# The modulation's side products in a two-branch mixer kernel: two channel tiles at every second large product instead of one at every product

## The chip, the cores and the metric

The kernel runs on one core of a Trainium2 chip. The metric is device microseconds (us) of one execution from launch to end. The kernel before has been timed three times: median 3220.7 us, 3216.38 to 3223.29 us.

A core has five engines with an instruction stream each: TensorE (PE in the profile, with its weight loads as PEld), VectorE (DVE), ScalarE (ACT), GpSimd (POOL) and SyncE (SP, which here issues nearly all DMAs). They wait for each other through semaphores. TensorE writes its results to PSUM, from where DVE and ACT fetch them.

## The reference, cut to what matters

Two layers over 384 tokens (128 of a prompt, 256 of a sample) with 2048 channels. In each layer the conditioning vectors give shift, scale and gate of the layer ("the modulation"), the normalised input goes through one large input projection, two branches mix the tokens, and a merged output projection ends the layer:

```python
mod_ctx = (jax.nn.silu(c_ctx) @ w_mod[l] + b_mod[l])[None]
mod_lat = jax.nn.silu(c) @ w_mod[l] + b_mod[l]
shift, scale, gate = jnp.split(mod, 3, axis=-1)
h = rms_norm(x, lp['g_pre']) * (1 + scale[:, None]) + shift[:, None]
(r, k, v, z_a, wlo_f, wlo_b, alo_f, alo_b, q_b, k_b, v_b, z_b, beta_in, alpha_in,
 gate_a_in, gate_b_in) = split_in_proj(h @ lp['w_in'])
# branch A: RWKV-7, 16 heads of 64, both directions     branch B: gated DeltaNet, 8 heads of 128
merged = sigmoid(gate_a_in) * branch_a + sigmoid(gate_b_in) * branch_b
out = merged @ lp['w_o']
x = x + gate[:, None] * rms_norm(out, lp['g_post'])
```

What the change concerns is `silu(c) @ w_mod[l]`: a product of two vectors (prompt and sample) with a matrix of 2048 x 6144 per layer.

## The kernel before

Large products take float32 operands as two float16 parts and multiply in three passes. A slab of 128 output channels of a weight matrix (1 MB, tile `st`) is loaded by SP, split into two `w` tiles by ACT and DVE (L228 to L230), and multiplied as 16 contraction tiles by 3 passes, 48 matmuls into a PSUM tile `jps`. `dense` (L446) goes through such tasks one after the other, always with the next slab loaded and split ahead, and calls `side_step(steps)` when a task's products have been issued.

The modulation is the side work that `side_step` (L349) takes up. `mod_third` (L277) is a generator for a third of it (shift, scale or gate of one layer). Each of its first 32 steps takes a `wm` tile (512 KB, two buffers, L347), issues its load (L285), and multiplies the 128 channels in it with the two conditioning vectors: four matmuls, each with a stationary `cpad` of 32 columns and 256 float32 columns streaming, into four 32-row groups of the PSUM tile `acc`. After the 32 steps ACT copies `acc` to a `wm` tile (L292); for thirds 0 and 1 four transposes follow, for third 2 the gate's rows go through DVE (L301, L302) to DRAM. 128 such steps are taken beside the large products: third 2 of layer 0, thirds 1 and 0 of layer 1 during layer 0, and third 2 of layer 1 during layer 1. In layer 0 61 tasks of branch A and 38 of branch B carry a step. `side_step(1000)` at the end of branch B takes whatever is left.

Branch A works through eight pairs of heads (0 to 7 below). Each has many short dependent products, written as generators too (`rwkv_front`, `rwkv_corner`, `rwkv_back`, `rwkv_out`); branch B has the same form with one head at a time. TensorE's order is made by `weave` (L91) as the program is written. It keeps a clock `now`, which every emitted matmul moves on by a planned cost (`mm`, columns / 2.4 ns, four times as much for float32, so 427 ns for a matmul of the side work). A generator yields how long its results need (HOP 1100, EVAC 2000, 3 * HOP and so on) or an event's name, and is taken up again when `now` is past that; in between come products of the `dense` tasks, which look up every second contraction tile. So side work on TensorE moves the generators' places. The orders of ACT, DVE, POOL and SP follow from a scheduler that works from priorities and dependencies, and which PSUM buffer a tile gets is settled there too; `tps`, the tile of most short products, has two.

Names in the rows: `k`, `r`, `v` are a pair's projections. `bones,sq` sums k's squares per head, `rs` is the inverse root of it (DVE L172, then POOL L173), `ident,rs` spreads it over the channels, `kk` (DVE L639) is k normalised, `lo,wup` are low-rank decays, `u` their evacuation on ACT (L651). `ivw`, `ivt` are the inversion of 32 x 32 blocks on DVE (L542 to L554), 60 short operations and two transposes to `nA` and `iva`. `nA,xc`, `iva,GA` and `v,revh` are products with the inverses and with v. In branch B `S,KQ`, `rt,Uf`, `vh,ktok`, `vn,QK` are the steps of the scan.

Of the kernel before, what the change touches and what calls it, by code (L numbers as in the profile page):

```python
# [24 lines left out]
# Large products: float32 operands are split exactly into float16 high and low parts after a power-of-two scaling;  # L25
# three passes (high high, high low, low high) carry float32's accuracy. Powers for weights, layer input, branches, merged.
SW, SX, SY, SM = 14, 6, 4, 4
# What TensorE's threads allow for, in ns: one answer of another engine (and a slower one, in those), a slab's way out of
# PSUM, convolution, decays, the first decays of branch B, inversions.
HOP, HOP_V, EVAC, CONV, DECAY, FIRST_B, INVERT_A, INVERT_B = 1100, 1.2, 2000, 8000, 7000, 3000, 37000, 48000  # L30
# Threads' ranks for the other engines; contraction tiles between two looks for a thread that can go on.
RANKS, STEP = (2000, 1000, 0, 0, 0, 0), 2
# By layer. Merge gates' channel tiles by pair of heads (and after the last) in branch A, by pair in branch B; branch A's
# projection by pair; the first heads of branch B that the last tiles of it take along; whole tiles left for the end.
# [5 lines left out]
# the order of the last outputs (block, slab), the residual's steps and those of the next input, by block  # L40
LAST = ("o00 o01 r0 r0 r0 o10 r0 o11 r1 r0 r1 o20 n0 r1 o21 r1 r2 n0 r2 n0 r2 r1 n0 r2 w0 w1 n1 n1 r2 w0 n2 n2 n2 "
        "n0 n0 n1 n1 n2 p0 n2 n2 w0 n0 n0 n0 n1 n1 n2 p0 n2 n2 w1 n0 n0 n0 n1 n1 n2 p0 p1 n2 n2 w1 p0 p1 p1 p1")
# channel tiles of the first modulation's pieces; the columns of the slabs that are multiplied piece by piece
# [7 lines left out]
def backbone(ctx: ExitStack, tc: tile.TileContext, i, o):  # L51
# [20 lines left out]
    # Work with many short dependent products is emitted by threads (generators). What a thread yields is the time, by the  # L72
    # cost of the products emitted meanwhile, that its results need before its next products, or the name of an event.
# [17 lines left out]
    def weave(threads, last):  # L91
        """Emits the threads' work; of those that can go on, the first does."""
# [33 lines left out]
    # each half reversed  # L126
# [5 lines left out]
    # sums the four groups of 32 rows  # L132
# [71 lines left out]
    def flag():  # L204
        """The column that takes a low part's sum: neither infinite (overflow) nor tiny everywhere (underflow)."""
        n = n_flag[0]
        n_flag[0] += 1
        return flags[:, n:n + 1]

    def run(fast):  # L210
# [21 lines left out]
        def weights(*srcs):  # L232
            """srcs [k 128, n] in DRAM -> their parts [128, all k, n] on chip"""
            return finish(weights_in_steps(*srcs))
# [22 lines left out]
        def product(ps, lhs, rhs, nk, ks=None):  # L257
            """ps += sum over k (of ks among nk) of lhs(part, k)^T rhs(part, k), in passes"""
            for kt in ks or range(nk):
                for n, (a, b) in enumerate(passes):  # L260
                    mm(ps, lhs(a, b, kt), rhs(a, b, kt), start=(kt == 0 and n == 0), stop=(kt == nk - 1 and n == len(passes) - 1))
                if kt % STEP == STEP - 1:
                    yield 0

        def finish(g):
            """runs a thread alone; its result"""
            try:
                while True:
                    next(g)
            except StopIteration as e:  # L270
                return e.value

# [4 lines left out]
        def mod_third(l, st, third, take):  # L277
            """One third of the modulation, half by half of its columns; take() gives the tile that they are loaded to."""
# [14 lines left out]
            if third == 2:  # L293
                # the gate's row, with the post-norm's weights, by streams
# [24 lines left out]
        def mod_piece(l, st, k0, k1, take):  # L319
            """Some channel tiles of shift and scale."""  # L320
# [27 lines left out]

        def side_step(n=1):  # L349
            while n and side:  # L350
# [7 lines left out]
        mods, pars = [], []  # L358

        def params(l):  # L360
# [25 lines left out]
            # halves; the rows of the output gates take the scale of their inputs as well  # L386
# [5 lines left out]
            # shift, scale by [channel, third, tile, stream]  # L392
# [4 lines left out]
        def norm_scale(ss):  # L397
            """ss[:, 0] = the norm's scale from two halves' sums of squares"""
# [6 lines left out]
        def scales(par, mod, ks):  # L405
            """the modulation's scales with the pre-norm's weights, in place"""
            V.scalar_tensor_tensor(out=mod[:, 1, ks], in0=mod[:, 1, ks], scalar=1.0, in1=bc(par[:, R_GPRE:R_GPRE + KT][:, ks], 2), op0=ADD, op1=MULT)

        def first_input(xT, par, mod, xs, kt):
            """layer 0: modulated channel tile, all tokens"""  # L410
# [5 lines left out]
        def layer(l, par, cw, hpar, omka, xs, ready, next_start, after):  # L416
# [5 lines left out]
            def by_channel(ws, n=128):  # L422
                """[channel, token] of a slab"""
# [6 lines left out]
            def by_token(ws):  # L430
                """[token in block, (block, channel)] of a slab"""
# [7 lines left out]
            def dense(tasks):  # L439
                """tasks: (slab, work with its parts); the next slab is loaded and split ahead"""  # L440
# [7 lines left out]
            def gate_tile(n):  # L448
                """tanh of half a channel tile of the merge gates, kept in DRAM"""
# [17 lines left out]
            # [token in block, (dir, head), block]  # L467
            beta, g, neg, vhs, al, ab = (lay.tile([128, 16, 3], F32, tag=t, name=t) for t in ("beta", "g", "neg", "vhs", "al", "ab"))
            # e^{cumulated g}; the same with the two chunks of a block swapped; e^{g left to the chunk's end}; e^{sum} of each chunk
# [18 lines left out]
            def decays():  # L488
# [34 lines left out]
                # neg: -e^g (forward), -beta e^g (backward); vhs: beta ekd (forward), ekd (backward)  # L523
# [7 lines left out]
            def silu2(ps, bufs=2):  # L531
                """2 silu(x) / cx from x / cx in PSUM"""
# [5 lines left out]
            def invert(pool, n_t):  # L538
                """n_t [128 = 4 quadrants of 32 rows, 32 blocks, 32]: minus a strictly upper N (row, column).
                Returns (a1, a2): a1[row, block, column] = (I + N)^-1, in n_t's place, and a2 its transpose, block by block."""  # L540
# [16 lines left out]
            # ================= branch A: RWKV-7, two heads per channel tile =================  # L557
# [4 lines left out]
            def lora(n):  # L562
                """a slab of the four low-rank inputs, each 96 channels"""
# [34 lines left out]
            def rwkv_tasks(hp):  # L598
                """the pair's projections; what a thread may still read is not overwritten before"""
# [19 lines left out]
            def rwkv_front(hp):  # L619
# [25 lines left out]
                # Z by chunk: rows of the solution (until then the k part of its right-hand side) and of the values  # L645
                kds, dirs, Zs = [], [], []
                for d in range(2):
# [28 lines left out]
                    # [channel, block, slot, 64]; slots of the even chunk then of the odd one:  # L676
                    # AR: r alpha | alpha r, BK: k b | b k; the backward direction has alpha, b and k reversed in time
# [27 lines left out]
                    # masked scores [row slot s, head, parity, block, t]: GA for alpha's columns, GR for r's  # L705
# [37 lines left out]
                # inverses: 32-blocks (the corner of each 64-block follows)  # L743
                a1, a2 = invert(P, nA)
                event(("inverse", l, hp), INVERT_A)
                # bonus: sum over the head's channels of r k r_k, both directions
# [12 lines left out]
            def rwkv_corner(hp):  # L759
# [3 lines left out]
                # the inverses of the 64-blocks, negated  # L763
# [22 lines left out]
            def rwkv_back(hp):  # L786
# [6 lines left out]
                # chunk by chunk; y takes the place of a chunk's alpha and r  # L793
# [78 lines left out]
                # bonus, group norm over the head, gate  # L872
# [665 lines left out]
```

## Time and profile before

| | |
|---|---|
| median of three runs | 3220.7 us (3216.38 to 3223.29) |
| the profiled execution, first to last instruction | 3223.1 us; it lists no time around this span |
| mean granted clock of TensorE | 0.969 |
| PE busy | 3009.9 us, 93% |
| DVE, ACT, POOL busy | 2325.1 (72%), 1461.4 (45%), 136.2 us (4%) |
| DMA | 457.89 MB, 142 GB/s in the mean |

The busy times are those of each engine alone, and overlap. TensorE is busy nearly always, so the span is TensorE's own work plus the short times in which it waits. Branch A of layer 0 lies at about 137 to 930 us, its branch B at 930 to 1470, branch A of layer 1 at 1690 to 2490 (with side work to 2096).

### The profile page before, as it was taken

The numbers are of one execution on the slowest core, as the hardware profiler recorded it, in microseconds if no ns is written. First come the engines' busy times: TensorE is split into PE (matmuls) and PEld (weight loads), VectorE is DVE, ScalarE is ACT, GpSimd is POOL, SyncE is SP. The second block draws the span as 40 slices with busy tenths as digits, with TensorE's granted clock in tenths as the row PEclk, the third lists the DMA queues.
The fourth block names the chain that finished last, engine by engine and source line by source line (L and its number), as shares of the span: only waits on it lengthen the run. The fifth ranks groups of instructions, "written<-read, shape, count | busy, mean of one in ns | idle before, by whom it ended". The sixth has DMA issues, their size and how long they took to land. (4 is left out here: it accounts for less than half of the span.)

```text
span 3223.1 us, 70249 instructions
## 1 busy us (share of the span) xinstructions
PE 3009.9 (93%) x28531; PEld 1990.2 (62%) x28531; DVE 2325.1 (72%) x6012; ACT 1461.4 (45%) x3144; POOL 136.2 (4%) x198
## 2 busy tenths in 40 slices
PE   6899999999999999997979999999999999999798
PEld 2466666666665555554976666666666655565388
DVE  3268888888867876765354788887887778887544
ACT  3344444444444555443355444444443446564332
POOL 1000000000000000000000000000000000000000
PEclk8999999999999999998989999999999999999899
DMA  9854444444465335467455545433334442335555
GB/s 342 263 147 132 125 126 133 140 131 139 135 173 159 108 113 159 139 185 201 126 158 156 141 132 149 114 99 91 98 106 123 118 127 71 106 89 167 152 150 160
DMA packets 659018, 457.89 MB, mean 142 GB/s; under 512 B 28858, under 2 KB 627708, under 8 KB 657148
## 3 DMA queue, kind: packets, MB, share of 16 engines
q1 hardware_dynamic: 658684, 453.30, 48.8%
q8 instruction: 227, 3.72, 0.5%
q14 instruction: 107, 0.88, 0.1%
HBM read 421.74 MB, written 31.49 MB: 141 GB/s over the span
## 5 line engine op out<-in xcount | busy, mean ns | idle before, releaser
L78 PE MATMUL jps<-x,w 128*128 128x384 f16 x8640 | 1534.3, 329 | 14.3 <-ACT x L228 7.9
L78 PEld LDWEIGHTS <-w 128*128 128x128 f16 (+1 forms) x10368 | 974.8, 99 | 735.0 <-issue 119.6
L230 DVE SCALAR_TENSOR_TENSOR w<-st,w 128x1024 f16<-128x1024 f32 (+3 forms) x574 | 643.9, 1128 | 239.5 <-ACT w L228 236.5
L228 ACT ACTIVATE w<-st 128x1024 f16<-128x1024 f32 (+3 forms) x574 | 556.3, 978 | 529.4 <-PE jps L78 333.6
L78 PE MATMUL cps<-w,mg 128*128 128x128 f16 x4608 | 265.0, 221 | 11.0 <-ACT mg L228 4.7
L78 PEld LDWEIGHTS <-mg 128*128 128x128 f16 x4608 | 263.6, 99 | 12.7 <-ACT mg L228 5.2
L549 DVE TENSOR_TENSOR ivw<-ivw,ivt 128x30 f32<-128x30 f32 (+4 forms) x720 | 237.6, 330 | 16.4
L547 DVE TENSOR_TENSOR ivt<-ivw 128x30 f32<-128x30 f32 (+4 forms) x720 | 236.8, 329 | 15.7
L78 PE MATMUL jps<-yb,w 128*128 128x384 f16 x744 | 138.9, 337 | 23.1 <-ACT w L228 11.9
L78 PE MATMUL jps<-ya,w 128*128 128x384 f16 x768 | 141.5, 333 | 4.3 <-ACT Uf L1291 1.8
L78 PE MATMUL acc<-wm,cpad 128*32 128x256 f32 (+1 forms) x1664 | 125.6, 384 | 16.0 <-DMA wm<-in_w_mod 15.9
L78 PEld LDWEIGHTS <-x 128*128 128x128 f16 x2304 | 131.3, 98 | 12.7 <-issue 10.0
L78 PE MATMUL jps<-w,x 128*128 128x128 f16 x2304 | 137.1, 220 | 0.0
L867 ACT COPY AR<-cps 64x128 f32<-64x128 f32 x192 | 49.9, 260 | 168.1 <-PE cps L78 163.5
L78 PE MATMUL tps<-AR,BK 64*128 64x128 f32 x768 | 119.0, 288 | 1.3 <-DVE GR L717 1.1
L1340 ACT ACTIVATE os<-cps,gx 64x128 f32<-64x128 f32 x160 | 57.9, 362 | 135.3 <-DVE rt L1338 132.9
L78 PEld LDWEIGHTS tps<-AR,BK 64*128 64x128 f32 x768 | 94.8, 187 | 20.0 <-issue 9.5
L840 DVE COPY Z<-cps 64x128 f32<-64x128 f32 x192 | 55.3, 288 | 60.6 <-PE cps L78 56.8
L730 ACT ACTIVATE nA<-GA 32x192 f32<-32x192 f32 x128 | 46.1, 360 | 108.0 <-DVE GA L715 106.7
L857 DVE SCALAR_TENSOR_TENSOR sring<-cps,pl,sp 64x64 f32<-64x64 f32 x256 | 72.4, 283 | 19.7 <-PE cps L78 15.4
L78 PEld LDWEIGHTS acc<-wm,cpad 128*32 128x32 f32 x1664 | 36.2, 110 | 71.2 <-issue 42.3
L1375 DVE SCALAR_TENSOR_TENSOR S<-S,gx,cps 128x128 f32<-128x128 f32 x128 | 39.1, 343 | 55.7 <-PE cps L78 55.3
(354 smaller groups left out, 3598.8 us busy)
## 6 DMA issues: line engine op xcount, KB each, us to landing
st<-in_w_in SPq DMA_DIRECT2D x194, 1024.0 KB
wm<-in_w_mod SPq DMA_DIRECT2D x176, 512.0 KB
st<-in_w_o SPq DMA_DIRECT2D x32, 1024.0 KB
st<-in_w_pa SPq DMA_DIRECT2D x32, 512.0 KB
gates<-gt SPq DMA_DIRECT2D x64, 192.0 KB
ms<-gates SPq DMA_DIRECT2D x64, 192.0 KB
st<-in_w_pb SPq DMA_DIRECT2D x36, 256.0 KB
wm<-in_w_mod SPq DMA_DIRECT2D x32, 256.0 KB
```

Of the source, the lines that this page charges most:

```text
L78: PE.matmul(out, lhsT=lhsT, rhs=rhs, start=start, stop=stop, **kw)
L228: S.activation(out=dst[0], in_=src, func=AF.Copy, scale=scale)
L230: V.scalar_tensor_tensor(out=dst[1], in0=src, scalar=scale, in1=dst[0], op0=MULT, op1=SUB, accum_out=flag())
L547: V.tensor_tensor(out=tv, in0=W[:, j + 1:32, j:j + 1].to_broadcast([128, n, j]), in1=W[:, j:j + 1, 0:j].to_broadcast([128, n, j]), op=MULT)
L549: V.tensor_tensor(out=W[:, j + 1:32, 0:j], in0=W[:, j + 1:32, 0:j], in1=tv, op=ADD)
L730: S.mul(nA[rq, 6 * d:6 * d + 6, :].rearrange("p (h b) t -> p h b t", h=2), GA[rq, :, p, :, 32 * q:32 * q + 32], -1.0)
L840: V.tensor_copy(dirs[d][4][ar, b, p, :], pb[ar, 0:128])
L857: V.scalar_tensor_tensor(out=sn[hs, hs], in0=pb[hs, o0:o0 + 64], scalar=plc[hs], in1=sp[hs, hs], op0=MULT, op1=ADD)
L867: S.copy(AR[rr, b, 2 * p:2 * p + 2, :].rearrange("p a b -> p (a b)"), pas[d][rr, 0:128])
L1340: S.activation(out=os_[d][R_, b, :], in_=pas[d][R_, 0:128], func=AF.Copy, scale=egs[R_, x, b:b + 1])
L1375: V.scalar_tensor_tensor(out=new[d], in0=cur[d], scalar=glast[:, p, x, b:b + 1], in1=pas[d][:, 128:256], op0=MULT, op1=ADD)
```

## The change

`side_step` now counts the steps that it is asked for in `owed`, returns while fewer than two are owed, and else takes all of them at once. Nothing else in the program differs (comments and docstrings are gone too, and lines behind the change are numbered higher by 7).

```diff
+        owed = [0]
+
         def side_step(n=1):
+
+            owed[0] += n
+            if owed[0] < 2:
+                return
+            n, owed[0] = owed[0], 0
             while n and side:
                 try:
                     next(side[0])
                     n -= 1
                 except StopIteration:
                     side.pop(0)
```

The same 512 matmuls of the side work stand in TensorE's order (before: 128 groups of four; now: 62 groups of eight and four of four). A pair of heads has seven tasks with a step, so from one pair to the next the groups fall behind other tasks.

The first place is TensorE in pair 3 of layer 0, from the sum of k's squares to the low-rank decays. Before:

```order
L78 MATMUL tps<-bones,sq 128x2 x3
L78 LDWEIGHTS w_4429
L78 MATMUL jps<-x_198,w_4429 128x384
...
L78 MATMUL tps<-ident,rs 64x128 x6
...
L78 MATMUL acc<-wm,cpad 32x256 x4
L78 LDWEIGHTS x_198
L78 MATMUL jps<-w_4494,x_198 128x128
...
L78 MATMUL tps<-lo,wup 128x384 x2
```

And now:

```order
L78 MATMUL tps<-bones,sq 128x2 x3
L78 LDWEIGHTS w_4429
L78 MATMUL jps<-x_198,w_4429 128x384
...
L78 MATMUL acc<-wm,cpad 32x256 x8
L78 MATMUL tps<-ident,rs 64x128 x6
L78 MATMUL tps<-lo,wup 128x384 x2
L78 LDWEIGHTS x_198
L78 MATMUL jps<-w_4488,x_198 128x128
```

Before, 24 large matmuls stand between `bones,sq` and `ident,rs`, then six, the side step and six more ahead of `lo,wup`. Now 18 large matmuls and two side steps stand ahead of `ident,rs`, and `lo,wup` follows it at once. Pairs 1, 5 and 7 read like 3; in pairs 2, 4 and 6 the side steps stand elsewhere, and 12 large matmuls and 42 more lie between `ident,rs` and `lo,wup`.

The second place is DVE at the same time, around `kk`. Before:

```order
L547 TENSOR_TENSOR ivt<-ivw 128x58
L639 SCALAR_TENSOR_TENSOR kk<-k,par,tps 128x384
L549 TENSOR_TENSOR ivw<-ivw,ivt 128x2x29
L547 TENSOR_TENSOR ivt<-ivw 128x30
L549 TENSOR_TENSOR ivw<-ivw,ivt 128x30
L553 STREAM_TRANSPOSE nA<-ivw 128x32x32
L554 STREAM_TRANSPOSE iva_4350<-ivw 128x32x32
L766 TENSOR_SCALAR Uf<-nA,m_122 128x12x32 x2
L230 SCALAR_TENSOR_TENSOR w_4578,flags<-st,w_4577 128x1024 x2
L659 SCALAR_TENSOR_TENSOR c_4599<-reset,u 128x384
```

And now:

```order
L554 TENSOR_TENSOR ivt<-ivw 128x58
L556 TENSOR_TENSOR ivw<-ivw,ivt 128x2x29
L554 TENSOR_TENSOR ivt<-ivw 128x30
L556 TENSOR_TENSOR ivw<-ivw,ivt 128x30
L560 STREAM_TRANSPOSE nA<-ivw 128x32x32
L561 STREAM_TRANSPOSE iva_4344<-ivw 128x32x32
L773 TENSOR_SCALAR Uf<-nA,m_122 128x12x32 x2
L230 SCALAR_TENSOR_TENSOR w_4569,flags<-st,w_4568 128x1024 x2
L646 SCALAR_TENSOR_TENSOR kk<-k,par,tps 128x384
L666 SCALAR_TENSOR_TENSOR c_4592<-reset,u 128x384
```

`kk`, which frees a `tps` buffer, has moved behind the end of the inversion, two transposes, two `Uf` and two splits of weights. It is so in pairs 1 and 3 of both layers.

The third place is TensorE at the end of layer 0's branch B. Before:

```order
L78 MATMUL cps<-S,KQ 128x128 x2
L78 MATMUL cps<-rt,Uf 64x128 x2
L78 MATMUL cps<-vn,QK 64x128 x2
L85 MATMUL tps<-swp,os 128x128 x3
L85 MATMUL tps<-ident,wm 128x128 x4
L78 LDWEIGHTS w_16662
L78 MATMUL jps<-yb_11081,w_16662 128x384
```

And now:

```order
L78 MATMUL cps<-S,KQ 128x128 x2
L78 MATMUL cps<-rt,Uf 64x128 x2
L78 MATMUL cps<-vn,QK 64x128 x2
L85 MATMUL tps<-swp,os 128x128 x3
L78 MATMUL acc<-wm,cpad 32x256 x4
L85 MATMUL tps<-ident,wm 128x128 x4
L78 LDWEIGHTS w_16634
L78 MATMUL jps<-yb_11093,w_16634 128x384
```

Layer 0 asks for 99 single steps, an odd number, so the last step of layer 1's third 0 is taken by `side_step(1000)`, and the transposes of this third stand right behind it.

## Rows read from the trace of the kernel before

**Rows 1.** The page: busy time, share of the span and instructions of each engine.
```profile
PE 3009.9 (93%) x28531; PEld 1990.2 (62%) x28531; DVE 2325.1 (72%) x6012; ACT 1461.4 (45%) x3144; POOL 136.2 (4%) x198
```

**Rows 2.** Windows by stage; columns are span, busy time per engine, PEclk, DMA share, GB/s.
```profile
137.00:930.00 793.00, 769.09 (x7484) 503.64 (x7485) 639.81 (x1640) 351.24 (x677) 38.75 (x39) 0.99 0.49 140
930.00:1470.00 540.00, 513.11 (x3958) 305.90 (x3956) 398.96 (x1055) 275.77 (x664) 22.30 (x22) 0.97 0.49 142
1690.00:2096.00 406.00, 394.57 (x3817) 260.52 (x3815) 310.18 (x775) 183.85 (x344) 18.09 (x30) 1.00 0.49 138
```

**Rows 3.** Tile `acc` on PE from 137 us: releaser, us of waiting, times.
```profile
  DMA wm<-in_w_mod: 2.2, 1
```

**Rows 4.** Timeline of PE: start, duration, instructions, [idle before, releaser].
```profile
400.30 7.97 PE L78 MATMUL jps<-x,w 128*128 128x384 f16 x48
408.20 0.64 PE L78 MATMUL acc<-wm,cpad 128*32 128x256 f32 x8
408.77 3.10 PE L78 MATMUL jps<-x,w 128*128 128x384 f16 x18
411.71 0.73 PE L78 MATMUL tps<-bones,sq 128*128 128x2 f32 x6
```

**Rows 5.** Timeline of PE early in layer 0: six side steps in a row.
```profile
87.51 2.80 PE L78 MATMUL acc<-wm,cpad 128*32 128x256 f32 x48
```

**Rows 6.** Waits of PE, 137 to 930 us: total us, times, longest.
```profile
PE tps L78 <- POOL rs L173: 6.7, 6, 1.3
PE tps L78 <- ACT v L609: 5.8, 7, 1.8
PE tps L78 <- ACT xc L775: 5.1, 12, 1.1
PE tps L78 <- DVE kk L639: 2.2, 6, 0.4
```

**Rows 7.** Timeline of PE in pair 3 of layer 0.
```profile
417.47 0.87 PE L78 MATMUL tps<-ident,rs 128*64 128x128 f32 x12 [1.11 <-POOL rs L173]
...
421.50 0.91 PE L78 MATMUL tps<-lo,wup 96*128 96x384 f32 x2 [0.36 <-DVE kk L639]
```

**Rows 8.** Timeline of DVE, the same stretch.
```profile
420.83 0.61 DVE L639 SCALAR_TENSOR_TENSOR kk<-k,par,tps 128x384 f32<-128x384 f32 x1
...
428.74 1.00 DVE L659 TENSOR_TENSOR_SCAN c<-reset,u 128x384 f32<-128x384 f32 x1
```

**Rows 9.** Timeline of ACT, the same stretch.
```profile
421.58 0.57 ACT L651 ACTIVATE u<-tps,hpar 128x384 f32<-128x384 f32 x1
```

**Rows 10.** Timeline of PE from layer 1's last side step on.
```profile
2095.60 0.63 PE L78 MATMUL acc<-wm,cpad 128*32 128x256 f32 x7
2096.74 0.24 PE L78 MATMUL tps<-nA,xc 32*32 32x32 f32 x2 [0.50 <-ACT xc L775]
...
2098.83 1.65 PE L78 MATMUL tps<-v,revh 128*128 128x384 f32 x2 [0.66 <-ACT v L609]
2100.27 2.07 PE L78 MATMUL jps<-x,w 128*128 128x384 f16 x6
```

**Rows 11.** Windows there, with the granted clock behind the five engines.
```profile
2098.00:2102.00 4.00, 3.34 (x18) 1.45 (x11) 2.47 (x4) 3.90 (x8) 0.00 (x0) 0.59 0.07 16
```

**Rows 12.** Timeline of PE in the next pair of layer 1, without side steps.
```profile
2176.21 0.88 PE L78 MATMUL tps<-ident,rs 128*64 128x128 f32 x12 [2.11 <-POOL rs L173]
...
2180.54 1.65 PE L78 MATMUL tps<-lo,wup 96*128 96x384 f32 x2 [1.50 <-DVE kk L639]
```

**Rows 13.** Timeline of PE in pairs 3 and 4 of layer 0, for comparison of durations.
```profile
418.27 1.15 PE L78 MATMUL jps<-x,w 128*128 128x384 f16 x6
...
525.81 0.91 PE L78 MATMUL tps<-v,revh 128*128 128x384 f32 x2 [0.66 <-ACT v L609]
```

**Rows 14.** Timeline of PE at the end of layer 0's branch B.
```profile
1462.89 0.90 PE L85 MATMUL tps<-swp,os 128*128 128x128 f32 x3 [4.75 <-DVE os L1398]
1464.50 1.12 PE L85 MATMUL tps<-ident,wm 128*128 128x128 f32 x4 [0.71 <-DVE yv L1410]
```

## The prediction

> **What bounds the kernel now.** I read the page's busy times first, then windows by stage, then the waits of TensorE and the timeline around the side steps. TensorE is busy 3009.9 of 3223.1 us [rows 1]. In branch A of layer 0 it idles 793.00 - 769.09 = 23.9 us, in branch B 540.00 - 513.11 = 26.9 us, in the part of layer 1 with side work 406.00 - 394.57 = 11.4 us [rows 2]; DVE, next, has 640 of 793 us. So a microsecond less on TensorE is one less at the end, as long as it doesn't come back as a wait. The loads of the 128 single side steps made TensorE wait once, 2.2 us [rows 3]: the side work costs its TensorE time, and hardly its transfers.
>
> **The switch.** 48 matmuls of a large product and one step take 408.77 - 400.30 = 8.47 us; 18 of these matmuls take 411.71 - 408.77 = 2.94 us, 0.163 each; so the step costs 8.47 - 48 x 0.163 = 0.63 us [rows 4]. (A step is 8 rows in the trace, two for each of its four matmuls.) Six steps in a row take 2.80 us; with 0.64 us for the first, each further one costs (2.80 - 0.64) / 5 = 0.43 us [rows 4, 5]. A pair thus costs 0.63 + 0.43 = 1.06 us instead of 1.26, 0.20 us less. A spacing smaller by 0.001 us, which these rows can't exclude, makes the step 0.68 us and the saving 0.25 us. 62 groups of eight: 62 x 0.20 = 12.4 us, to 62 x 0.25 = 15.5 us. Nothing covers this work, so all of it is on the path. I take 0.22 x 62 = 13.6 us. Bounds: 0 if what costs is not the entry but the following product's first weight load, which waits in any case, and 15.5.
>
> The Trainium skill, in "TensorEngine Tiling (Array Packing)", Key Properties, says that changing the tiling mode drains TensorE; a step goes from 128 x 128 to 128 x 32 and back, so it predicts two drains per group and agrees in sign with the rows above. Its size differs: from the drain of about 128 cycles in "TensorE: Matmul & The Clock Gate", Step-by-step, an estimate is 2 x 0.053 = 0.11 us per pair, 6.6 us in all, and the sum below would be about -2 us. The rows, which hold every cost of the entry, decide.
>
> **The inverse root and `kk`, branch A.** Before, `ident,rs` waits in pairs 1 to 7 for POOL (6 waits, 6.7 us) and the second `lo,wup` for `kk` on DVE (6, 2.2 us) [rows 6]; pair 3 shows 1.11 and 0.36 us [rows 7]. Now the groups alternate. In even pairs 54 large matmuls lie between `ident,rs` and `lo,wup`, 54 x 0.163 = 8.8 us, so the 0.36 us goes: five pairs in both layers, -1.8 us. In odd pairs `ident,rs` follows 18 large matmuls and two steps (2.93 + 1.06 = 4.0 us, where 24 matmuls took 3.9): the wait stays near 1.1 us, but `rs` now stands behind more of the inversion in DVE's order, and I allow 0.7 us more in three pairs, +2.1. `lo,wup` follows at once. `kk`, which ended at 421.44, has moved behind what ended at 428.74 in the trace [rows 8]. If the second `lo,wup` needed the buffer that `kk` frees, it would wait some 7 us. In pairs 1 and 3 of both layers the order gives it the buffer of the first `lo,wup`, which ACT frees with a 0.57 us operation [rows 9]; I take 0.67 us for each instead of 0.36, +1.3 us. In pairs 5 and 7 of layer 0 and pair 0 of layer 1 it does wait for `kk`, which stands behind 13 or 14 operations of the inversion and a split. No row prices that: it lies between the 1.50 us on `kk` where no side step fills [rows 12] and the 7.3 us of the whole move. Only a part of the inversion is ahead, so I stay near the first: 2.2, 2.7 and 1.5 us, less the 0.36 that was there, +5.3 us. Sum: -1.8 + 2.1 + 1.3 + 5.3 = +6.9 us. Bounds: -5 (all odd waits covered) and +35 (rival 3).
>
> **`v` and `xc`, branch A.** `nA,xc` and `v,revh` right behind a single step wait 0.50 and 0.66 us [rows 10], 5.1 and 5.8 us in all in layer 0 [rows 6]. Now in odd pairs large matmuls and `cps` work come between them (v's wait of 0.66 gone), in even pairs `v,revh` follows the group of eight at once: `v,revh` starts 2098.83 - 2095.60 = 3.2 us behind its product's end [rows 10], the group lasts 1.06, so some 2.1 us of wait in one against 1.2 in two before. Three pairs of that kind cost 2.7, the odd ones save 0.66 in five and some of xc's: -1 us in the sum; bounds -7 and +5.
>
> **The other places.** At the end of layer 0's branch B the last step now stands between `swp,os` and the transposes, with ACT's copy of `acc` in between. TensorE idles there already, 4.75 and 0.71 us [rows 14]; the step hides in the 0.71, the copy and its two hand-overs don't: +1 us (0 to 1.3). Pair 0 of layer 0 loses its filler ahead of `lo,wup`: +1, a wait of the size of the 1.11 us [rows 7]. In branch B a step between two dependent scan products covers 0.63 us of a wait, a pair 1.06 in half as many places; no row prices the difference, so I take -2, with bounds of a third of the idle time there [rows 2], -9 and +9. Loads: two 512 KB transfers now follow each other where one did, at a DMA share of 0.49 [rows 2], and each still has two tasks' time (2 x 8.47 = 17 us) [rows 4] ahead of its use: 0, and if this cover goes, up to a wait like the 2.2 us now and then. SP's other issues are only passed by one transfer.
>
> **The clock.** Behind the cluster of waits at 2096 to 2099 us the granted clock is 0.59 over 4 us, a mixture of 1.2 and 2.4 GHz [rows 11], and the two `v,revh` and six large matmuls take 1.65 and 2.07 us [rows 10] against 0.91 and 1.15 [rows 13]: such a spell costs 0.74 + 0.92 = 1.7 us. Longer single waits in odd pairs may add some and removed clusters save some: 0, bounds -5 and +8 (three spells fewer, five more).
>
> **Sum.** -13.6 + 6.9 - 1 + 1 + 1 - 2 = -7.7 us, -8 rounded, on a span of 3223.1 us, which lies 2.4 us above the median. Median: 3220.7 - 8 = 3213 us.
>
> **Rivals.**
> 1. The saving in full. The waits moved in odd pairs are covered and the twelve short waits of `xc` and `v` shrink: -13.6 - 5 = -19, 3202 us. For it: TensorE's waits on these lines are only 20 us in layer 0's branch A [rows 6], so little can be lost. Against: the order shows `kk` later in seven pairs.
> 2. The saving eaten. Waits of 3 us more in each of the seven pairs where `kk` is late, 21 us in place of the 6.9, or fewer with spells of 1.7 us behind them: -7.7 + 14 = +6 at the most, near 0 in the middle, 3221 us. For it: where a pair has no side step as filler, the waits are 2.11 and 1.50 us [rows 12] and the second one runs at the lower clock (1.65 us for the product of 0.91). The Trainium skill's "TensorE: Matmul & The Clock Gate", on a second failure mode, describes TensorE losing its clock through frequent short idle times between groups; the trace agrees behind clusters such as that of rows 10.
> 3. Slower. `kk` behind the transposes holds up TensorE itself: `kk` is also what the rest of the pair's front needs, and a TensorE product standing in the fixed order ahead of large ones waits for it, at 428.74 - 421.44 = 7.3 us in each of pairs 1 and 3 of both layers, 29 us, plus four spells of 1.7: +36, less 13.6 and with 4.6 us from the other terms: +27, 3248 us. It decides as soon as the `tps` buffer at run time is the one that `kk` frees, or a scan product waits for the decays behind it. For it: 7.3 us is no small move; against: the order's waits name ACT there.
> 4. The change doesn't do what it says, or the cost of a step is in its matmuls alone: groups of eight are there in the order, but 0.63 + 0.63 remains; then +5.9 from the rest, 3227 us.
>
> **How the numbers follow.** Forecast 0.50 (own range 3205 to 3221), rival 1 0.16, rival 2 0.16, rival 3 0.12, rival 4 0.06. A change under 0.2%, 6.4 us, can't be told from none: 3214.3 and 3227.1 are the bounds. Faster: all of rival 1 and six tenths of the forecast, 0.16 + 0.31 = 0.47. Slower: rival 3, a third of rival 4 and tails of the forecast and of rival 2, 0.12 + 0.02 + 0.05 = 0.19. Same: the other 0.34. The range reaches from rival 1's far side, 3196, into rival 3, which reaches down to about 3236 if half of its waits are covered; about 0.08 is left out above and 0.05 below.
>
> **What would show it.** In the profile after: groups of sixteen `acc` rows whose start to the next large product is 1.06 us (1.26 for rival 4); PE's waits on `rs` near 8 us in layer 0's branch A, and on `kk` at most three of 2 to 3 us, in pairs 5 and 7 of layer 0 and pair 0 of layer 1; the 2.2 us wait for `wm` still single; `ident,wm` about 1 us later behind `swp,os`. Branch A of layer 0 should be 4 us shorter or more, the side part of layer 1 2 us. Waits near 7 us on `kk` would prove the forecast wrong (rival 3), and so would a step that costs the same in a pair, or a lower mean clock than 0.969 by more than 0.005.

## The result, and the profile after

The changed kernel takes 3259.9 us in the median (3254.06 to 3261.62, 4 runs), the kernel before 3222.0 us on the same chip (3216.38 to 3228.16, 4 runs): a ratio of 1.0119, 95% interval 1.01 to 1.0139. It is slower by 38 us where 8 us less were forecast, outside of the range given. The profiled executions span 3259.6 and 3223.1 us.

The stages, each from the start of one product to that of the next in the timeline of TensorE, show where the 36.5 us between these two lie:

| from, to | before, us | after, us | difference |
|---|---|---|---|
| start, `bones,sq` of pair 0, layer 0 | 140.8 | 139.9 | -0.9 |
| pair 0 | 85.5 | 87.0 | +1.5 |
| pairs 1 to 6 (to `bones,sq` of pair 7) | 554.0 | 574.3 | +20.3 |
| pair 7 to the first `swp,os` of branch B | 314.2 | 314.8 | +0.6 |
| branch B to its last `swp,os` | 368.4 | 375.2 | +6.8 |
| to `bones,sq` of pair 0, layer 1 | 255.8 | 258.2 | +2.4 |
| layer 1, pairs 0 to 3 | 357.6 | 361.9 | +4.3 |
| the rest | 1146.8 | 1148.4 | +1.6 |

Most of the loss is in the parts that have side work, and over half of it in pairs 1 to 6 of layer 0. The windows of TensorE for that stage (columns as in [rows 2]), first the kernel before, then the one after:

```profile
226.32:780.28 553.96, 535.52 (x5328) 354.55 (x5327) 468.65 (x1207) 248.69 (x487) 30.28 (x30) 0.99 0.46 132
```
```profile
226.91:801.17 574.26, 542.33 (x5329) 364.27 (x5328) 466.93 (x1205) 249.11 (x487) 31.77 (x30) 0.96 0.45 127
```

TensorE is idle 13.5 us longer (31.93 instead of 18.44), and *busy* 6.8 us longer with the same products, at a granted clock of 0.96 instead of 0.99. Where it waits, the waits of TensorE from 137 to 950 us in the kernel after say (columns as in [rows 6], which they answer to):

```profile
PE tps L78 <- ACT v L616: 12.0, 3, 4.8
PE tps L78 <- DVE kk L646: 5.7, 2, 2.9
PE tps L85 <- DVE y L898: 5.2, 4, 2.8
PE tps L78 <- POOL rs L173: 4.3, 6, 1.5
...
PE tps L78 <- ACT xc L782: 2.5, 2, 2.3
PE tps L78 <- ACT u L658: 2.0, 3, 0.7
```

Many waits of about 1 us have become a few of 2 to 5 us. The longest are those on `v`. One line is new: the transposes of the branch's output (`ident,y`) wait for `y` from DVE, 5.2 us here and 3.6 us in layer 1, where before neither stretch shows such a wait. The timeline of TensorE in pair 4, where `v,revh` before waited 0.66 us [rows 13]:

```profile
509.62 0.80 PE L78 MATMUL tps<-bones,sq 128*128 128x2 f32 x6
...
519.84 1.51 PE L78 MATMUL tps<-lo,wup 96*128 96x384 f32 x4
521.18 5.86 PE L78 MATMUL jps<-w,x 128*128 128x128 f16 x102
526.97 1.07 PE L78 MATMUL acc<-wm,cpad 128*32 128x256 f32 x16
532.88 1.65 PE L78 MATMUL tps<-v,revh 128*128 128x384 f32 x2 [4.84 <-ACT v L616]
```

The product that gives v ends at 526.97. The group of eight follows, and `v,revh` at once behind it waits for 4.84 us. The timelines of ACT and of DVE say why:

```profile
529.65 0.52 ACT L671 ACTIVATE pe<-c 128x384 f32<-128x384 f32 x1 [6.01 <-DVE c L666]
530.57 0.52 ACT L672 ACTIVATE u<-u 128x384 f32<-128x384 f32 x1 [0.39 <-DVE u L669]
531.00 0.51 ACT L673 ACTIVATE c<-c 128x384 f32<-128x384 f32 x1
531.41 1.04 ACT L228 ACTIVATE w<-st 128x1024 f16<-128x1024 f32 x1
532.36 0.47 ACT L616 ACTIVATE v<-jps 128x384 f32<-128x384 f32 x1
```
```profile
524.37 1.98 DVE L560 STREAM_TRANSPOSE nA<-ivw 128x1024 f32<-128x1024 f32 x1
526.20 1.98 DVE L561 STREAM_TRANSPOSE iva<-ivw 128x1024 f32<-128x1024 f32 x1
528.05 0.70 DVE L773 TENSOR_SCALAR Uf<-nA,m 128x384 f32<-128x384 f32 x2
528.68 0.94 DVE L666 TENSOR_TENSOR_SCAN c<-reset,u 128x384 f32<-128x384 f32 x1
```

In ACT's order v's evacuation stands behind four operations and the first of them waits 6.01 us for `c` on DVE, which stands behind the end of the inversion and its transposes. So v can't be had before about 532.8, 5.9 us behind its product. The plan allows it 2.0 us (EVAC) and counts the group of eight as 3.42 us, so it puts nothing else ahead of the waiting product. Against the kernel before, both sides have moved: measured from the pair's `bones,sq`, v's product ends 17.4 us behind it instead of 19.3, and `c` starts 19.1 us behind it instead of 17.0.

Other places as they came out: a pair of side steps costs what was worked out. On the pages of the two profiles the busy time of the side matmuls falls from 125.6 to 112.2 us, and from these rows of TensorE's timeline a pair takes 507.66 - 499.74 - 42 x 0.163 = 1.07 us:

```profile
499.74 6.99 PE L78 MATMUL jps<-x,w 128*128 128x384 f16 x42
506.65 1.07 PE L78 MATMUL acc<-wm,cpad 128*32 128x256 f32 x16
507.66 2.12 PE L78 MATMUL jps<-x,w 128*128 128x384 f16 x12
```

In pair 5 the second `lo,wup` waits for `kk`, as forecast, and the product behind the wait runs at the lower clock (compare [rows 7]); at the end of branch B the transposes stand 2.64 us behind `swp,os` instead of 1.61 [rows 14]:

```profile
618.01 1.65 PE L78 MATMUL tps<-lo,wup 96*128 96x384 f32 x2 [2.81 <-DVE kk L646]
...
1491.12 0.90 PE L85 MATMUL tps<-swp,os 128*128 128x128 f32 x3 [4.75 <-DVE os L1405]
1491.95 1.08 PE L78 MATMUL acc<-wm,cpad 128*32 128x256 f32 x8
1493.76 1.11 PE L85 MATMUL tps<-ident,wm 128*128 128x128 f32 x4 [0.73 <-ACT wm L292]
```

### The profile page after: what moved, and what is told of

Its sections match the earlier page's. It is cut to its first block, busy times and chain, and to the rows that moved or that the text cites. A ratio compares the mean times of both kernels' runs of the same rounds, so it can differ in the third digit from the quotient of the medians.

```text
span 3259.6 us, 70243 instructions
## 1 busy us (share of the span) xinstructions
PE 3017.2 (93%) x28531; PEld 2010.5 (62%) x28531; DVE 2326.1 (71%) x6012; ACT 1461.1 (45%) x3144; POOL 140.8 (4%) x198
## 5 line engine op out<-in xcount | busy, mean ns | idle before, releaser
L78 PE MATMUL cps<-w,mg 128*128 128x128 f16 x4608 | 263.7, 221 | 11.4 <-ACT mg L228 4.6
L78 PE MATMUL acc<-wm,cpad 128*32 128x256 f32 (+1 forms) x1664 | 112.2, 379 | 11.7 <-DMA wm<-in_w_mod 7.9
L1004 DVE TENSOR_TENSOR og<-cps,gp 128x128 f32<-128x128 f32 x96 | 27.7, 288 | 71.0 <-ACT junk L1003 71.0
```

Of the source, the lines that this page charges most:

```text
L78: PE.matmul(out, lhsT=lhsT, rhs=rhs, start=start, stop=stop, **kw)
L1004: V.tensor_tensor(out=og[:, b, 128 * d:128 * d + 128], in0=t[:, 0:128], in1=gp[:, stream_of(b), 128 * d:128 * d + 128], op=MULT)
```

## The experiments

Theory 1: the loss comes from the *places* of the generators' products in TensorE's order. The planner counts a group of eight as 8 x 427 ns = 3.42 us, and it lasts 1.06; so the planner takes results for ready that aren't yet. Theory 2: it comes from multiplying in pairs itself (filler gone from every second place, loads two at a time). Theory 3: any other order moves the time by some tens of us, without a rule. Ratios are to the kernel before, run on the same chip in turns, with 95% intervals.

### The same places, the other grouping

These four settle the main question. Each keeps one kernel's order of all products but the side work, and groups the side work the other way. For that the side matmuls count nothing in the plan (`cost=0.0`), and `side_step` moves the planner's clock itself:

```diff
# h1, h2: single steps, planned as pairs        # h3, h4: pairs, planned as single steps
# (cut to the lines that matter)
+  owed[0] += 1                                 +  if n == 1 and plan:
+  owed[1] += plan.pop(0) if plan else 0.0      +      now[0] += plan.pop(0)
+  if owed[0] == 2:                                owed[0] += n
+      now[0] += owed[1]                           if owed[0] < 2:
+      owed[:] = 0, 0.0                                return
```

In the traces TensorE's order is indeed the same, but for some neighbouring small products that change places and, in h3 and h4, six large matmuls that have moved to another place. DVE's and ACT's orders are not held: they follow from the scheduler and differ somewhat between the two groupings.

> Single steps as before the change, while the planner's clock stands still at the first of two tasks that ask for a step and moves by 3414 ns at the second, so all other products stand as in the changed kernel in both layers. If the places cost the 38 us: 3245 to 3275 us (3260, with 13.6 more for the switches and some waits less where a step now fills). If multiplying in pairs costs them: 3218 to 3232 us.

> Single steps at the places of the run with pairs at the real price (3201 us). If each order is tuned to the grouping for which it was planned, whichever that is: slower, 3210 to 3230 us. If the switch saving of pairs reaches the end: 3201 + 13.6 = 3215 us. If grouping makes no difference at equal places: 3198 to 3205 us.

> Pairs at the places of the kernel before, now in layer 1 as well. As in the first run of that kind (3227 us, where layer 1's places differed): the switch saving turns into waits, 3215 to 3228 us. If the first run lost it to layer 1's places: 3205 to 3213 us.

> Pairs at the places of the single steps with the real price (3199.6 us), now in layer 1 as well. If the 30 us of the first run of that kind were partly layer 1's places: 3205 to 3222 us. If pairs cost that much at these places: 3225 to 3235 us.

| places of the other products | single steps | pairs |
|---|---|---|
| of the kernel before (427 ns a side matmul) | 1 (3222 to 3225 us) | 1.0025 [1.0011, 1.0039], 3230.3 us |
| of the changed kernel (427 ns, in pairs) | 1.0119 [1.0101, 1.0137], 3263.6 us | 1.0119 [1.01, 1.0139], 3259.9 us |
| planned for single steps at 160 ns | 0.9919 [0.9898, 0.994], 3199.6 us | 1.001 [0.9999, 1.002], 3226.5 us |
| planned for pairs at 132 ns | 0.9945 [0.9924, 0.9965], 3207.5 us | 0.9928 [0.9906, 0.995], 3201.3 us |

At the changed kernel's places single steps are as slow as pairs (inside the 3245 to 3275 us expected of the places), and pairs at the places of before are hardly slower than single steps (3230.3 us, a little above the 3215 to 3228 expected). So the places cost the 38 us, and theory 2 falls for this change. In the third row pairs do lose, as h4's second answer has it (3225 to 3235 us); in the fourth none of h2's three answers was met (3207.5 us). The trace of the single steps at the changed places has the same waits on v, 3 of up to 4.2 us, here behind a step of 0.64 us in pair 4:

```profile
524.97 0.64 PE L78 MATMUL acc<-wm,cpad 128*32 128x256 f32 x8
529.78 1.44 PE L78 MATMUL tps<-v,revh 128*128 128x384 f32 x2 [4.17 <-ACT v L617]
```

Down the columns 60 us lie between the best and the worst places. Along the rows pairs gain at most 0.2% and lose up to 0.9%, and the 13.6 us (0.42%) saved on switches are not to be seen in any; only the fourth row's intervals, of two runs on different chips, would leave room for them. Two earlier runs of the last form kept the places in layer 0 only (the plan was shifted in layer 1), and came out alike:

> The side steps are multiplied in pairs as in the changed kernel, but the planner's clock is moved by 1707 ns at each task that asks for a step (as before the change) and by nothing when the pair is issued, so the generators' products stand at the same large products as before the change. Theory 1 (the loss comes from the new places of the generators' products, behind which DVE's inversion and ACT's queue are late): the switch saving stays and the waits are near those of before: 3222 - 13.6 + up to 5 for filler missing in odd pairs = 3208 to 3214 us, faster than before. Theory 2 (pairing itself costs: filler gone from every second place, loads in bursts): 3240 us or more, slower than before.

> The side steps in pairs, while the planner's clock moves by 640 ns at each task that asks for a step, as in the run with single steps at the real price (3199.6 us), so the generators' products keep that run's places. If the 0.22 us that a pair saves reaches the end where TensorE waits little: 3199.6 - 13.6 = 3186 us. If each pair's saving turns into a wait again, as in the first run with places kept: 3198 to 3202 us.

The first gave 1.0014 [1.0, 1.0029], 3227.1 us, the second 1.0011 [0.9999, 1.0022], 3230.0 us. In neither did one of the two answers hold. Where the saving goes is seen in the first. From pair 1 to pair 7 of layer 0 it takes 554.7 us, the kernel before 554.0. In the windows of that stage TensorE is busy 6.0 us less than before (529.6 instead of 535.5; the side work itself 22.1 instead of 26.2), and its idle time rises from 18.4 to 25.2 us. For the run with the same layer 0 order (h3) the waits there, under those of before:

```profile
PE tps L78 <- POOL rs L173: 5.6, 5, 1.3
PE tps L78 <- ACT v L609: 5.1, 6, 1.8
PE tps L78 <- ACT xc L775: 4.3, 10, 1.1
PE tps L78 <- DVE kk L639: 1.8, 5, 0.4
PE cps L78 <- DVE Z L840: 0.8, 2, 0.5
```
```profile
PE tps L78 <- POOL rs L173: 6.6, 6, 1.6
PE tps L78 <- ACT v L619: 5.3, 6, 2.0
PE cps L78 <- DVE Z L850: 3.9, 5, 1.1
PE tps L78 <- DVE kk L649: 3.4, 3, 1.2
PE tps L78 <- ACT xc L785: 3.2, 6, 1.2
```

A step that stood ahead of a waiting product hid up to 0.64 us of its wait, and where it is gone, the wait is longer: `Z,BKT` in pair 1 waits 1.11 us in h3, and 0.54 us in the kernel before, where a step stands shortly ahead of it. That this accounts for all of the lost saving is not shown.

### The planned price

> The changed kernel, with the planner told the real price of a side matmul in a pair (132 ns instead of 427). Theory 1 in its narrow form (the group of eight is planned at 3.42 us and lasts 1.06, so v,revh and others come 2.4 us too early): the 4.8 us waits on v shrink to about 2.5 and the time falls to 3225 to 3240 us. Theory 1 in its wide form (DVE's inversion sets when v and the decays are ready, wherever the planner puts the rest): 3245 to 3260 us. Theory 2: 3255 to 3262 us.

> The kernel before the change, with single steps, but the planner is told what a step's matmul really takes (160 ns instead of 427). Theory 1: places move as they do in the changed kernel (lo,wup 24 products later in each pair, v,revh 12 products later), so the time moves by more than 0.3% without any pairing; with the waits of the changed kernel's even pairs it would be 3235 to 3255 us. Theory 2: no pairing, no loss: 3222 us within 8.

> The changed kernel with the planned price of a side matmul half way between the real one (132 ns, 3201 us) and the old one (427 ns, 3260 us). Theory 1 (a price too high brings the generators' products too early): between the two, 3215 to 3245 us. Theory 3 (any other order moves the time by some 30 us either way, without a rule): as likely outside of 3201 to 3260 as inside, or beside one of the ends.

> Single steps, with a planned price of 853 ns a matmul, so a single step counts 3.41 us in the plan, as a group of eight does in the changed kernel. Theory 1: products come too early without any pairing, and in twice as many places: 3245 to 3290 us. Theory 2 (pairing itself costs): 3222 us within 10. Theory 3: no rule.

> The changed kernel with a planned price below the real one (54 ns, so a group of eight counts 0.43 us and lasts 1.06). Theory 1 says that only products that come too early cost a wait; too late costs little as long as nobody else waits for them: 3195 to 3215 us. If the place alone counts, whichever way it is off: 3215 to 3235 us. Theory 3: no rule.

> Single steps at a planned price between the real one (160 ns, 3199.6 us) and that of the kernel before (427 ns, 3225 us). Theory 1: between them, 3203 to 3221 us. Theory 3: no rule.

The edit in each is one number, in `mod_third`'s call of `mm` (`now[0] += cost` in place of the rule by columns):

```diff
-  start=(kt == 0), stop=(kt == KT - 1))
+  start=(kt == 0), stop=(kt == KT - 1), cost=132.0)
```

Why 427 ns is too much shows in the trace of the kernel before: a row of the side work lasts 379 ns in the median, yet the eight rows of a step take 0.64 us together, since the four matmuls, which write to four different row groups of `acc`, run side by side. The planner adds them up.

| planned ns a side matmul | grouping | planned, real us a group | time, us | ratio |
|---|---|---|---|---|
| 54 | pairs | 0.43, 1.06 | 3241.1 | 1.0057 [1.0038, 1.0075] |
| 132 | pairs | 1.06, 1.06 | 3201.3 | 0.9928 [0.9906, 0.995] |
| 280 | pairs | 2.24, 1.06 | 3227.3 | 1.0009 [0.9997, 1.0021] |
| 427 (the change) | pairs | 3.42, 1.06 | 3259.9 | 1.0119 [1.01, 1.0139] |
| 160 | single | 0.64, 0.63 | 3199.6 | 0.9919 [0.9898, 0.994] |
| 290 | single | 1.16, 0.63 | 3230.0 | 1.0023 [1.0008, 1.0037] |
| 427 (before) | single | 1.71, 0.63 | 3222 to 3225 | 1 |
| 853 | single | 3.41, 0.63 | 3312.1 | 1.0261 [1.0241, 1.028] |

With the real price the changed kernel gains 58 us, more than any of the three expectations allowed (3225 us and up), and beats the kernel before. The kernel before gains 0.8% in the same way, where theory 1 as written down expected a loss of the moved places. Planned at what a group of eight counts in the changed kernel, single steps lose 2.6%, more than the 3245 to 3290 us expected: no pairing is needed for the loss. For pairs the time rises in order from 132 to 280 to 427 ns, and it rises below the real price too: of what g1 was to tell, that products that come too late cost little is refuted (3241 us), and 3241 is even above the range of the other answer. 290 and 427 ns for single steps stand in the wrong order, 290 above 427, where 3203 to 3221 us were expected. So the price moves the time, by up to 110 us, and the real one is the best of those tried for either grouping. What it doesn't explain, the 40 us below the real price and a scatter of about half a per cent, is left to theory 3. The waits on v are gone at the real price (the two greatest of TensorE's waits in the run with pairs at 132 ns, 137 to 930 us), and the window of pairs 1 to 6 is shorter by 38 us than the changed kernel's, at full clock:

```profile
PE tps L78 <- POOL rs L173: 4.1, 3, 1.9
PE tps L78 <- ACT u L658: 2.7, 4, 0.7
```
```profile
226.74:762.69 535.95, 524.39 (x5327) 354.24 (x5327) 453.76 (x1184) 248.41 (x486) 26.35 (x30) 1.00 0.48 136
```

How the waits on v went is more than theory 1 says, which speaks of TensorE alone. Pair 4 in that run, on TensorE, DVE and ACT:

```profile
493.63 0.73 PE L78 MATMUL tps<-bones,sq 128*128 128x2 f32 x6
...
513.35 0.81 PE L78 MATMUL tps<-v,revh 128*128 128x384 f32 x2
```
```profile
507.19 0.95 DVE L666 TENSOR_TENSOR_SCAN c<-reset,u 128x384 f32<-128x384 f32 x1
...
519.38 2.01 DVE L561 STREAM_TRANSPOSE iva<-ivw 128x1024 f32<-128x1024 f32 x1
```
```profile
512.38 0.47 ACT L616 ACTIVATE v<-jps 128x384 f32<-128x384 f32 x1
```

TensorE comes to `v,revh` 19.7 us behind `bones,sq`; in the changed kernel it stood there waiting from 18.4 us on, and in the kernel before it came at 21.9. So it is later than in the changed kernel by 1.3 us only. The greater part is DVE's: `c` starts 13.6 us behind `bones,sq` instead of 19.1, and v leaves ACT 4.0 us sooner. `c` now stands in the middle of the inversion and no longer behind its end. In pairs 2 to 7 the inversion ends 9 to 19 us behind `c` at the real price (both groupings), while it ends ahead of `c` in all six pairs before and in five of six after the change. The planner allows the inversion 37 us of its own clock (INVERT_A); a clock that runs ahead lets these pass sooner, and the products that need the inverses stand earlier. That DVE's order follows from this is our reading; no run changed it alone.

### The pairs at other tasks

> The changed kernel with one step owed from the start, so that every pair falls on the neighbouring task (planned price 427 ns as in the changed kernel). Theory 1 (price): the groups are still planned at 3.42 us and last 1.06, now in the other pairs of heads: 3245 to 3275 us. Theory 3 (the order's luck, no rule): anything from 3200 to 3275 us.

> The same shift by one task, with the real price of 132 ns. Theory 1: within 10 us of the run with pairs at the real price, 3192 to 3212 us. Theory 3: anything from 3200 to 3260 us.

The edit is `owed = [1]` for `owed = [0]`, in the changed kernel and in the one with the real price. They gave 3267.2 us (1.0144 [1.0124, 1.0164]) and 3218.6 us (0.9989 [0.9979, 0.9998]). The first is as theory 1 has it, though theory 3 allowed it too. The second misses theory 1's 3192 to 3212 us and lies where theory 3 allowed it: with the real price the shift by one task costs 17 us, so e1's 3201 us was in part a lucky place. The gap between the two prices remains, 48.6 us here and 58.6 us without the shift. So theory 3 is not refuted as a part of the time; it gives no reason for the gap.

### The wait on v, and what it costs

> The changed kernel, with only the plan for v changed: its result is counted on 3.4 us later (EVAC + 3400 ns for v), so that v,revh stands 12 to 24 large matmuls behind the group of eight. Theory 1: the three v waits of 12 us in all in layer 0's branch A fall to some 5 us and the half-clock stretches behind them go too (17 us of them at 350 and 732 us, worth half): 3236 to 3250 us. If the waits only move to another product of the same pair (nA,xc or iva,GA): 3255 to 3265 us. Theory 2: 3255 to 3262 us.

> The changed kernel, with useless large matmuls ahead of v,revh in the pairs where it waits: 26 (4.2 us) in pairs 4 and 6 of layer 0 and 4 of layer 1, 12 (2.0 us) in pair 2 of both; they are nearly as long as the waits of 4.84 and 2.33 us, and their results are overwritten. If the waits cost more than their length because the clock falls behind them: the half-clock stretches at 350, 541 and 732 us (27 us) and at 1958 and 2146 (7 us) go, and the time falls by 7 to 14 us, to 3246 to 3253 us. If the lower clock costs nothing, 3259 to 3263 us, since the waits' length stays.

```diff
# e4                                                             # f4, ahead of mm(t[:, 0:T], revh, v); abridged
- event((c, l, hp), EVAC)                                        + for _ in range(12 or 26):
+ event((c, l, hp), EVAC + (3400 if c == "v" else 0))            +     PE.matmul(t[:, 0:T], lhsT=xs[0][:, 0, 0:128], rhs=xs[0][:, 0, :], ...)
```

Moving v alone gave 3249.6 us (1.0066 [1.0044, 1.0088]), 10 us better (17 by the two ratios), in the range of theory 1. The execution that was profiled is the slowest of the five, 3262.9 us, so its trace doesn't show what gained the 10 us. It does show where the waits went: from 150 to 900 us those on v are out of the first five, and `iva`, which the inversion gives, is waited for instead:

```profile
PE tps L78 <- DVE iva L561: 8.3, 3, 3.1
PE tps L78 <- DVE kk L646: 5.6, 2, 2.8
```

So the time that v takes isn't all that is wrong: in that execution TensorE waits 8.3 us for `iva`, which stands next in the pair, where it waited 12.0 us for v.

Filling the waits with useless products gave 3242.4 us (1.0047 [1.0031, 1.0062]), 17.5 us less than the changed kernel (0.7%, or 23 us, by the two ratios, which compare on one chip each) and better than the 7 to 14 expected, though nothing came ready sooner: `v,revh` starts 527.33 - 521.39 = 5.94 us behind v's product, in the changed kernel it was 5.91. TensorE in pair 4:

```profile
521.39 1.07 PE L78 MATMUL acc<-wm,cpad 128*32 128x256 f32 x16
522.39 4.40 PE L700 MATMUL tps<-x 128*128 128x384 f16 x26
527.33 0.91 PE L78 MATMUL tps<-v,revh 128*128 128x384 f32 x2 [0.54 <-ACT v L616]
```

The windows of 8 us behind the wait, in the changed kernel and with the wait filled, then that of pairs 1 to 6 with the wait filled:

```profile
532.00:540.00 8.00, 7.12 (x88) 4.03 (x90) 3.81 (x7) 5.15 (x10) 0.00 (x0) 0.67 0.50 130
```
```profile
526.50:534.50 8.00, 7.46 (x128) 4.61 (x127) 7.64 (x13) 5.93 (x12) 2.01 (x1) 1.00 0.50 129
...
226.90:789.70 562.80, 542.17 (x5393) 366.01 (x5392) 466.89 (x1205) 248.88 (x487) 29.41 (x30) 0.99 0.46 130
```

The granted clock behind the wait is 1.00 (2.4 GHz) instead of 0.67 (a mixture with 1.2 GHz), and the stage takes 562.8 us instead of 574.3. So of the 20.3 us that the change lost there some 11 are not waits but products at the lower clock behind them. That agrees with the sum from the windows: busy +6.8 us, although 21 pairs of side steps save 21 x 0.22 = 4.6 us, makes 11.4 us of slower products.

## Why the prediction was wrong, point by point

The forecast put the waits at +5.9 us, the clock at 0 and the switch at -13.6. Over the whole span TensorE's idle time rose by 29.2 us (from 213.2 to 242.4), and its busy time by 7.3 us (3009.9 to 3017.2) although the side work is busy 13.4 us less: the other products took 20.7 us more, at a mean granted clock of 0.961 instead of 0.969. So two terms failed, the waits by 23 us and, as far as the slower products are its doing, the clock by 21. A mean clock lower by more than 0.005 was among the signs that the prediction itself gave of being wrong.

- *The switch* was right: 1.07 us a pair, and 13.4 us less of TensorE's time in the side work where 13.6 were forecast. The estimate from the drain in the Trainium skill's "TensorE: Matmul & The Clock Gate", Step-by-step, 0.11 us a pair, was half of what the trace shows (with it the prediction's sum would have been about -1, not -2 us). But "all of it is on the path" was wrong: at places kept equal, pairs gained nothing beyond 0.2% (e3, f5, h1 to h4).
- *`rs` and `kk`*: +6.9 us was forecast for both layers, within wide bounds, and the parts came out otherwise. In layer 0 `kk` waits twice for 2.81 and 2.88 us in pairs 5 and 7 (2.2 and 2.7 were forecast), and `u` three times for 0.67 us, as forecast in pairs 1 and 3. `rs` fell to 4.3 us instead of rising. From 137 to 950 us the three lines sum to 12.0 us, against 8.9 before [rows 6]: +3.1. In layer 1 they fell by 1.6 us, and the wait on `kk` forecast for its pair 0 didn't come. The 54 matmuls between `ident,rs` and `lo,wup` were priced too high: 42 of them stream 128 columns and take 0.057 us each (102 in 5.86 us in the timeline of pair 4), not 0.163; the wait that they were to cover went all the same. The 7.3 us on which rival 3 rested never came; its sum (3248 us) was nearest to the result, but `kk` was not what held TensorE up. What did is kin to its other condition, the late decays: v's evacuation stands in ACT's queue behind them.
- *`v` and `xc`* is the step that failed first: -1 us was forecast, +5.0 came (+3.6 in layer 0, +1.4 in layer 1), at the edge of its bounds. It took the 3.2 us from v's product to `v,revh` out of the trace as if they were a property of v. They are set by the place of `c` in DVE's order, to which ACT's queue is tied, and with `c` later and TensorE earlier they became 5.9 us. The waits in pairs 2, 4 and 6 are 2.34, 4.84 and 4.85 us where 2.1 each were forecast, and those of 2.32 and 4.84 us in pairs 2 and 4 of layer 1 are like them; the forecast had counted three such pairs, not five.
- *Lines without a term*: the waits of `ident,y` on `y`, 8.8 us in the two branches A, stand nowhere in the forecast, and in layer 0's branch A of the run with pairs at the real price (137 to 930 us) they don't show.
- *The clock* is the step with the largest error in layer 0: 0 us was forecast, 11.5 us are measured for pairs 1 to 6. The trace of before has waits of up to 1.8 us in that stage and 10 us at the lower clock; the changed kernel has waits of 2.3 to 4.85 us and 44 us at the lower clock, 14 with the waits on v filled. The bound of +8 us for the whole kernel was passed in this stage alone. No run prices a single spell, so the 1.7 us taken for one stays open.
- *Branch B*: -2 us was forecast, +6.8 us came, inside the bounds. One wait of 6.14 us on `iva` shows there, where before the longest on it was 3.62, and 4.1 us on `ga`, before 0.9. That the places are its cause is borne out by single steps at the changed places, which have it as well (5.73 us on `iva`); more was not tested.
- *The loads* were no cost: `acc` waited for no load of `wm` in the kernel after, from 137 us on.
- *The end of branch B*: +1 was forecast, the transposes came 1.03 us later.

What the forecast didn't see is, as far as the runs show, common to these points. It went through the new places one by one and priced each by a wait that the trace of before shows. It didn't ask how the places had been chosen: by a plan that counts a side matmul at 427 ns, which rows of the trace (0.64 us for four) refuted from the start. Grouping more than doubled that error at one place, from 1.08 to 2.36 us, and a group planned at 3.42 us is longer than the 2.0 us that the plan allows for a result such as v, so the product that waits for it follows with nothing else ahead of it.

Open are two things. One is why the places planned for single steps at 160 ns bear pairs so badly: 0.9919 to 1.001, of which pairs 1 to 6 hold 7 of the 30 us between the two profiled executions; that DVE's order differs between them is one candidate. The other is why a price below the real one costs 40 us. The traces tell where: of the 43 us between the profiled executions at 54 and 132 ns, 13 lie in pairs 1 to 6 and 22 behind pair 3 of layer 1, where next to no side work is left.

## What to carry to other kernels

Where an order is written by a planner, a change moves what the planner counts, and that can cost more than the change saves: compare its prices with the trace first, here one number that was worth 0.8% in the kernel before and 1.5 to 1.8% in the changed one. To tell grouping from places, keep the plan's clock as it was and change only what is emitted. The time that a result takes in one trace is no property of it where another engine's queue stands in between: look for what stands ahead of it there. And a wait of several us on TensorE is to be priced with the products behind it, which run at the lower clock.

## What the runs showed of the hardware

A gap of 4.84 us in TensorE's work was followed by a stretch with a granted clock of 0.67 over 8 us, and useless products in the gap kept it at 1.00; in the stage that has three such gaps (2.34, 4.84 and 4.85 us) filling them was worth 11.5 us, nearly the 12.0 us of the waits themselves. Four float32 matmuls of 256 columns, each with 32 stationary columns and a row group of PSUM of its own, took 0.63 us between large products and 0.43 us behind another four: they run side by side. What a second step behind the first saves was the same 0.20 us with any order: in pairs 1 to 6 of layer 0 the side work is busy 26.2 us with single steps (the kernel before, e2, h1), and 22.1 us with pairs (the changed kernel, e1, e3, h3, h4, f4).
